# Attention scores of a prompt as fp32r products over 128 rows, with the high and low parts of queries and keys stacked in the halves of the array, in one layer of a hybrid decoder

## The chip, the cores and the metric

The kernel runs on one core of a Trainium2 chip. The metric is the time of one execution on the device in microseconds (us). Five engines appear in the profile: TensorE (PE, with its weight loads as PEld), VectorE (DVE), ScalarE (ACT), GpSimd (POOL) and SyncE (SP). SP and POOL also issue most of the DMA transfers. L135 in a row of the profile is line 135 of the kernel.

## The reference

One inference step of one trunk layer, all in float32: 512 prompt tokens and 8 x 8 sample tokens of width 1024, so 576 columns in all. Cut to what matters:

```python
h = _rmsnorm(x, norm1_g) * (1.0 + sc1) + sh1           # sc, sh, g: silu(c) @ w_ada + b_ada
proj = h @ w_in                                        # B, C, x, q, k, v, two gates
u = c_gate * xa
uc, new_conv = _causal_conv(u, conv_buf, conv_w)
ya = (b_gate * uc) @ w_conv_out
o, k_state, v_state = attend(q, k, v, attn_sinks)      # window 128, 4 key heads x 4 query heads of 64
yb = o @ w_attn_out
mixed = sigmoid(ga) * ya + sigmoid(gb) * yb
x = x + g1 * (mixed @ w_mix_out)
h2 = _rmsnorm(x, norm2_g) * (1.0 + sc2) + sh2
a, val = split(h2 @ w_up); ac, new_ffn = _causal_conv(a, ffn_buf, ffn_conv_w)
x = x + g2 * ((gelu(ac) * val) @ w_down)               # y = final norm of x

# inside attend, prompt, for each block of 128 queries against its own and the previous block of keys:
s = einsum('...qhgd,...khd->...hgqk', q, k) * HEAD_DIM ** -0.5
s = s - slopes * dist                                  # masked outside the window
m = max(max(s), sink); p = exp(s - m); p = p / (sum(p) + exp(sink - m))
o = einsum('...hgqk,...khd->...qhgd', p, v)
```

The change concerns the first line of attend for the prompt: sums over 64 channels of a head.

## The kernel before

The kernel is one Tile program. A scheduler places the instructions of each engine with a timing model of its own, except those of engines that are pinned to the order in which they are written: PE is pinned from ahead of the attention to the end, ACT and DVE from the fifteenth job (`N_ATT`) on. Helpers record most instructions in one place, so most rows have line 135.

**Large products.** A float32 product is made of three fp32r products: each operand is split into a high part (ACT copies to fp32r, `whi`, `hh`) and a low part (DVE subtracts, `wlo`, `hl`), and high·high, high·low and low·high are added in PSUM. After the first normalisation, the keys and the first query tile (`kT`; the first query tile bears that name too), and the value projection `V`, the rest of the input projection and all later products form a list of jobs. A job has seven parts of 12 products of 128x288, accumulated in the PSUM banks `bx`, `bz` and `by`, in the order bx, bz, by, bx, by, bz, by. Three of the early jobs (1, 4 and 7) give the remaining query tiles. The weights come from DRAM in `raw` tiles (a ring of four, loaded by SP). For the second block of a job the low part is made without DVE: ACT copies the high part negated, and a DMA on POOL's queue adds `raw` to it (`wlo<-raw`). Most other tiles, `kT`, queries, scores, `pt`, and the modulation weights `ada`, live in one pool of 54 buffers; a tile takes the place that came free, and its writer waits for the readers of the tile before it.

**Attention runs as filler.** `attention` is a generator that `beside_conv` advances between the pieces of the jobs' products (`tick`, .28 of a step at each). It goes through 16 units (key head `hd`, block `i`). A unit has two pairs of query heads (x = 0, 1); a tile of queries and a tile of keys hold two heads each, in rows 0 to 63 and 64 to 127 (e = 0, 1). `prompt_scores` writes the scores, adds the distance term (DVE) and ends with the softmax (DVE and ACT). Two units later `prompt_turn` transposes the probabilities (`pt`), and with every second unit `prompt_values` multiplies the `pt` of two units with `V` (L1191). Behind the values stand products for the second half of the modulations: `Modulations.sums` takes four `ada` tiles at a time (`side_by_side`, L1290, `rows<-ada,cT`). A head's units do not begin before `ready`, that is `Q_TICKS` pieces after its queries are there.

In the program's names a product is written out<-moving,stationary. The scores before:

```python
for x in range(2):
    for e in range(2):
        matmul(
            S[e][:, x * 256 : x * 256 + w], QS[2 * hd + x][HALF[e], i * P : i * P + P],
            keys(hd, e)[:, k0 : k0 + w], start=True, stop=True,
        )
```

These are four plain float32 products with 64 rows, w = 256 keys wide (128 for the first block of a head). Keys must be in the same half as the queries, so `kX` holds the two key tiles with their halves swapped, by four DMAs on POOL's queue (L941). On that queue lie, ahead of the attention, also the stores of the last keys and values (L919 to L930), the sinks (`snk`, L969) and the loads of the filters and the final gain (`par`, L999).

Of the kernel before, what the change touches and what calls it, by code (L numbers as in the profile page):

```python
# [10 lines left out]
F32 = mybir.dt.float32  # L11
F32R = mybir.dt.float32r
AF = mybir.ActivationFunctionType
ALU = mybir.AluOpType
AX = mybir.AxisListType

P = 128
D = 1024
NK = D // P
SEQ = 512  # L20
# [10 lines left out]
MOD_AHEAD = 7  # L31
MOD_TICKS = 6
N_ATT = 14
Q_TICKS = 8
OPS_AT = 1, 2, 3, 4
CACHE_AT = 17
EPS = 1e-6
# [38 lines left out]
def step_kernel(ctx: ExitStack, tc: tile.TileContext, ins: dict, outs: list):  # L76
    nc = tc.nc
# [35 lines left out]
    def slot(s, dt=F32, shape=None):  # L113
        return ap_.tile(shape or [P, NT], dt, tag="a", name=nm(s))
# [7 lines left out]
    def aux():  # L122
        return pa.tile([P, 512], F32, tag="aux", name=nm("aux"))
# [18 lines left out]
    matmul, transpose = pe.matmul, pe.transpose  # L142
# [6 lines left out]
    def pv(t):  # L149
        return t[:, 0:512]  # L150
# [10 lines left out]
    def split(hi, lo, src):  # L161

        act.activation(hi, src, AF.Copy)
        dve.tensor_tensor(out=lo, in0=src, in1=hi.bitcast(F32), op=ALU.subtract)
# [47 lines left out]
    ticks = [0]  # L212
# [347 lines left out]
    par = cp.tile([88, P], F32, tag="par", name="par")  # L560
# [302 lines left out]
    kT = []  # L863
    for j in (2, 0, 1):
        t = slot("kT")
# [21 lines left out]
    for raw in raws:  # L887
        hi = wp.tile([P, 4, 256], F32R, tag="whi", name=nm("whi"), bufs=S_BUFS)
        lo = wp.tile([P, 4, 256], F32R, tag="wlo", name=nm("wlo"), bufs=S_BUFS)
# [31 lines left out]
    for i in (3, 4):  # L921
# [3 lines left out]
        t = slot("kout", shape=[P, 256])  # L925
# [9 lines left out]
    qS = slot("qS", shape=[P, 2, 2, 4, 2, 2, 8])  # L935
    qX = slot("qX", shape=[P, 2, 2, 4, 2, 8])

    KX = [slot("kX", shape=[P, 512]) for _ in range(2)]
    for x, t in zip(KX, kT):
        for par in range(2):  # L940
            nc.gpsimd.dma_start(x[HALF[1 - par]], pv(t)[HALF[par]])  # L941

    def keys(hd, par):

        return (kT if par == hd % 2 else KX)[hd // 2][HALF[par]]

    def queries(t, q):

        hd, g2 = t // 2, t % 2
        for par in range(2):  # L950
            mine = HALF[par]
            dst = qS[:, hd // 2, :, :, par, g2, :] if par == hd % 2 else qX[:, hd // 2, :, :, g2, :]
            nc.vector.tensor_copy(
                out=dst[mine], in_=sv(q)[mine].rearrange("p (q b t) -> p q b t", q=2, b=4)
            )
        QS[t] = q
        ready[hd] = ticks[0] + Q_TICKS
        if g2 == 1:
            par = 1 - hd % 2
            for q in range(2):  # L960
                nc.gpsimd.dma_start(
                    qS[HALF[1 - par], hd // 2, q, :, par, :, :].rearrange("p b g t -> p b (g t)"),
                    qX[HALF[par], hd // 2, q].rearrange("p b g t -> p b (g t)"),
                )
# [3 lines left out]
    tc.keep_in_program_order(  # L968
        nc.gpsimd.dma_start(snk, ins["attn_sinks"][0, :].partition_broadcast(P))  # L969
    )  # L970
    queries(0, q0)
    w_q1 = weights(kpm(w_in, Q0 + P), NK)
    nd = V[2][:, 1, :]
# [172 lines left out]
    def prompt_scores(hd, i):  # L1146
        w = 256 if i else P
        k0 = (i - 1) * P if i else 0
        ss = [slot("s", shape=[P, 2, 256]) for _ in range(2)]
        S = [aux() for _ in range(2)]  # L1150
        for x in range(2):
            for e in range(2):
                matmul(
                    S[e][:, x * 256 : x * 256 + w], QS[2 * hd + x][HALF[e], i * P : i * P + P],
                    keys(hd, e)[:, k0 : k0 + w], start=True, stop=True,
                )
        for x in range(2):
            for e in range(2):
                nc.vector.scalar_tensor_tensor(
                    out=ss[x][:, e, :w], in0=nd[:, 256 - w : 256],  # L1160
                    scalar=2.0 ** (-8.0 * (4 * hd + 2 * x + e + 1) / 16),
                    in1=S[e][:, x * 256 : x * 256 + w], op0=ALU.mult, op1=ALU.add,
                )
        softmax(ss, 4, snk[:, 4 * hd : 4 * hd + 4], nsnk[:, 4 * hd : 4 * hd + 4], w)
        return ss
# [40 lines left out]
    def attention(sums):  # L1206
        units = [(hd, i) for hd in range(4) for i in range(4)]
        s, pts = {}, {}
        for n in range(len(units) + 3):
            if n == CACHE_AT:  # L1210
                cache_load(0)
            if n < len(units):
                hd, i = units[n]
                while 2 * hd + 1 not in QS or ticks[0] < ready[hd]:
                    yield False
                s[n] = prompt_scores(hd, i)
            if n >= 4 and n % 2 == 0:
                prompt_values([(*units[u], pts.pop(u)) for u in (n - 4, n - 3)])
                sums()
            yield False  # L1220
            if 2 <= n <= len(units) + 1:
                pts[n - 2] = prompt_turn(units[n - 2][1], s.pop(n - 2))
            yield False
        filler[1] = .45
        before = None
        for n in range(3):
            s, more = [], []
            if n < 2:
                yield from decode_scores(n, s, more)
            if before is not None:  # L1230
                yield from before
            before = decode_values(n, s, more)
# [1090 lines left out]
```

## Time and profile before

| what | value |
|---|---|
| median of three runs | 966.89 us (966.0 to 967.5) |
| profiled execution | 964.89 us, of which the span is 963.1 us |
| PE busy | 943.6 us (98% of the span), 7346 instructions |
| DVE, ACT, POOL busy | 723.9, 571.9 and 141.1 us |
| units of scores | between 75 and 330 us of the span, beside the jobs |

The page names for each engine its busy time, its share of the span and its number of instructions, then the span in 40 slices, the DMA queues, the chain of waits that ended last, the costliest groups of instructions and the DMA issues. A float32 product appears as two records, an fp32r product as one. The ends of products on PE are modelled, so the starts of successive products say more than the durations. All numbers of a trace come from the one profiled execution; the runs' times are taken apart from it.

### The profile page before, as it was taken

Reading aid. Unit: us, or ns where it says so; the run is one execution under the profiler, and the core shown is the slowest. Engines: PE = TensorE matmul, PEld = TensorE weight load, DVE = VectorE, ACT = ScalarE, POOL = GpSimd, SP = SyncE. Lnnn points to the kernel's source line nnn. Section 1 sums busy time; section 2 is a strip of 40 time slices with the busy share of each in tenths; the row PEclk is TensorE's granted clock in tenths of the full one; section 3 lists DMA queues with packets and bytes.
Section 4 is the critical chain, followed back from the end, with each engine's and each line's share of the span. In section 5 each row is a group of like instructions: output and inputs, shape, how many; then the busy total and the mean of one; then the engine's idle time right before and its main releaser. Section 6 shows DMA issues by size and latency. Waiting matters only on the chain.

```text
span 963.1 us, 18913 instructions
## 1 busy us (share of the span) xinstructions
PE 943.6 (98%) x7346; PEld 900.1 (93%) x7346; DVE 723.9 (75%) x1368; ACT 571.9 (59%) x1088; POOL 141.1 (15%) x320
## 2 busy tenths in 40 slices
PE   6999999999999999999999999999999999999997
PEld 5799889798889998999999999999999999999997
DVE  5687977787767558776778688995559998868864
ACT  5366686666556655686555567563226565546664
POOL 2131112021111212212001131100000000001110
PEclk9999999999999999999999999999999999999999
DMA  9987577755675888999466732332333333328542
GB/s 276 329 266 191 150 217 201 240 134 156 189 216 121 191 216 232 240 247 254 155 197 159 175 96 67 88 109 68 108 90 88 88 89 100 93 69 178 135 95 99
DMA packets 194635, 154.32 MB, mean 160 GB/s; under 512 B 7896, under 2 KB 178716, under 8 KB 194258
## 3 DMA queue, kind: packets, MB, share of 16 engines
q1 hardware_dynamic: 181890, 113.81, 39.9%
q0 software_dynamic: 11360, 36.94, 17.7%
q10 hardware_dynamic: 1296, 2.36, 0.7%
q8 instruction: 57, 0.93, 0.4%
q14 instruction: 32, 0.26, 0.1%
HBM read 115.98 MB, written 14.17 MB: 135 GB/s over the span
## 4 chain that ended last, share of the span: by engine, by line
PE 93%; DMA 3%; ACT 2%; DVE 1%; SPq 1%; issue 1%; ACTq 0%; DVEq 0%
PE mm L135 34%; PE aux L135 25%; PE by L135 13%; PE bx L135 9%; PE bz L135 8%; PE rows L1290 2%; PE aux L1191 1%; DMA ad<-in_w_ada 1%; SPq L552 1%; DMA wlo<-raw 1%; DMA x<-in_x_prompt 0%; ACT whi L135 0%; ACT wlo L135 0%; ACT s L1030 0%; DVE g L135 0%
## 5 line engine op out<-in xcount | busy, mean ns | idle before, releaser
L135 ACT ACTIVATE whi<-raw 128x1024 fp32r<-128x1024 f32 (+3 forms) x192 | 194.7, 1023 | 113.9 <-PE bz L135 36.9
L135 DVE TENSOR_TENSOR wlo<-raw,whi 128x1024 fp32r<-128x1024 f32 (+3 forms) x153 | 180.6, 1185 | 30.6 <-ACT whi L135 28.6
L135 DVE TENSOR_TENSOR raw<-raw 128x512 f32<-128x512 f32 x100 | 70.1, 701 | 2.5
L135 PE MATMUL aux<-2h,whi 128*128 128x288 f32 (+2 forms) x232 | 68.6, 296 | 0.0
L135 PE MATMUL aux<-2h,wlo 128*128 128x288 f32 (+2 forms) x232 | 68.5, 295 | 0.0
L135 PE MATMUL aux<-2l,whi 128*128 128x288 f32 (+2 forms) x232 | 68.4, 295 | 0.0
L135 POOL DMA_DIRECT2D wlo<-raw x39 | 34.4, 882 | 184.8 <-ACT p L135 59.7
L135 PE MATMUL bx<-hh,whi 128*128 128x288 f32 x184 | 55.8, 303 | 0.0
L135 PE MATMUL bx<-hl,whi 128*128 128x288 f32 x184 | 54.4, 296 | 0.0
L135 PE MATMUL bx<-hh,wlo 128*128 128x288 f32 x184 | 54.3, 295 | 0.0
L135 PE MATMUL mm<-fh,whi 128*128 128x256 f32 x224 | 47.8, 295 | 0.0
L135 PE MATMUL mm<-fh,wlo 128*128 128x256 f32 x224 | 47.7, 294 | 0.0
L135 PE MATMUL mm<-fl,whi 128*128 128x256 f32 x224 | 47.1, 292 | 0.0
L135 PEld LDWEIGHTS aux<-2h,whi 128*128 128x128 f32 x232 | 43.6, 188 | 0.0
L135 PEld LDWEIGHTS aux<-2l,whi 128*128 128x128 f32 x232 | 43.6, 188 | 0.0
L135 PEld LDWEIGHTS aux<-2h,wlo 128*128 128x128 f32 x232 | 43.5, 188 | 0.0
L135 DVE SCALAR_TENSOR_TENSOR y<-pad,par2T,y 128x592 f32<-128x592 f32 x44 | 36.6, 833 | 9.0 <-ACT y L135 8.2
L135 ACT ACTIVATE wlo<-whi 128x1024 fp32r<-128x1024 f32 (+1 forms) x39 | 40.0, 1025 | 0.8
L135 PE MATMUL by<-t,whi 128*128 128x288 f32 x184 | 39.0, 303 | 0.9 <-ACT by L135 0.9
L135 DVE SCALAR_TENSOR_TENSOR x<-mm,modT,x 128x512 f32<-128x512 f32 (+2 forms) x26 | 17.2, 663 | 28.8 <-PE mm L135 28.8
L135 PE MATMUL bz<-t,whi 128*128 128x288 f32 x184 | 38.6, 300 | 0.0
L135 PEld LDWEIGHTS mm<-fh,whi 128*128 128x128 f32 x224 | 37.2, 188 | 0.2 <-ACT nh L135 0.2
(430 smaller groups left out, 3265.5 us busy)
## 6 DMA issues: line engine op xcount, KB each, us to landing
raw<-in_w_in SPq DMA_DIRECT2D x52, 512.0 KB, 5.0
raw<-in_w_up SPq DMA_DIRECT2D x44, 512.0 KB, 3.9
wlo<-raw POOLq DMA_DIRECT2D x33, 512.0 KB, 4.7
ada<-in_w_ada SPq DMA_DIRECT2D x64, 256.0 KB, 5.2
ad<-in_w_ada SPq DMA_DIRECT2D x32, 256.0 KB, 6.4
raw<-in_w_down SPq DMA_DIRECT2D x16, 512.0 KB, 4.0
sg_dram<-sg POOLq DMA_DIRECT2D x16, 288.0 KB, 5.6
gt<-sg_dram SPq DMA_DIRECT2D x16, 288.0 KB, 5.0
```

The lines of the kernel that those rows point to most:

```text
L135: done = getattr(self.engine, name)(*args, **kwargs)
L552: return tc.keep_in_program_order(nc.sync.dma_start(dst, src))
L1191: done = nc.tensor.matmul(O[HALF[par], c], vt(i - nkt + 1 + kt)[:, hd * 64 : hd * 64 + 64], pts[kt][:, par * 256 : par * 256 + 256], start ...
L1290: done = nc.tensor.matmul(ps[32 * j : 32 * j + 32, :], cT[:, k, :], cols[j][:, k % 2, :], start=(k == 1), stop=(k == NK - 2),)
```

## The change

The scores become fp32r products over all 128 rows. The keys of a head are split into a high and a low part, and each part is written to both halves of a tile (`key_parts`: for two heads six DMAs on POOL's queue in place of two, and the `kX` tiles go). The queries are split too, and high and low are stacked: `qh` holds the high part of the even head above its low part, `qo` that of the odd head (three DMAs for each tile of queries). A product of a stacked query tile with the high keys then gives (high + low)·high, one with the low keys (high + low)·low, and both are added in PSUM. A unit has eight such products in place of four plain ones, its scores stand in one PSUM tile for each x, and the parts of the second pair of key heads are made after the sixth unit. `Q_TICKS` goes from 8 to 10.

```diff
--- before.py
+++ after.py
@@ -31,7 +31,7 @@
 MOD_AHEAD = 7
 MOD_TICKS = 6
 N_ATT = 14
-Q_TICKS = 8
+Q_TICKS = 10
 OPS_AT = 1, 2, 3, 4
 CACHE_AT = 17
 EPS = 1e-6
@@ -935,25 +935,36 @@
     qS = slot("qS", shape=[P, 2, 2, 4, 2, 2, 8])
     qX = slot("qX", shape=[P, 2, 2, 4, 2, 8])
 
-    KX = [slot("kX", shape=[P, 512]) for _ in range(2)]
-    for x, t in zip(KX, kT):
-        for par in range(2):
-            nc.gpsimd.dma_start(x[HALF[1 - par]], pv(t)[HALF[par]])
-
-    def keys(hd, par):
-
-        return (kT if par == hd % 2 else KX)[hd // 2][HALF[par]]
+    KS = {}
+
+    def key_parts(j):
+
+        parts = [slot("k", F32R, [P, SEQ]) for _ in range(4)]
+        split(parts[0], parts[1], pv(kT[j]))
+        for x in range(2):
+            src, dst = (t.bitcast(F32) for t in (parts[x], parts[x + 2]))
+            for half in HALF:
+                nc.gpsimd.dma_start(dst[half], src[HALF[1]])
+            nc.gpsimd.dma_start(src[HALF[1]], src[HALF[0]])
+        KS[2 * j], KS[2 * j + 1] = parts[0:2], parts[2:4]
 
     def queries(t, q):
 
         hd, g2 = t // 2, t % 2
+        hi, lo, odd = (slot(n, F32R, [P, SEQ]) for n in ("qh", "ql", "qo"))
+        nc.scalar.activation(hi, pv(q), AF.Copy)
+        nc.vector.tensor_tensor(out=lo, in0=pv(q), in1=hi.bitcast(F32), op=ALU.subtract)
         for par in range(2):
             mine = HALF[par]
             dst = qS[:, hd // 2, :, :, par, g2, :] if par == hd % 2 else qX[:, hd // 2, :, :, g2, :]
             nc.vector.tensor_copy(
                 out=dst[mine], in_=sv(q)[mine].rearrange("p (q b t) -> p q b t", q=2, b=4)
             )
-        QS[t] = q
+        h32, l32, o32 = (x.bitcast(F32) for x in (hi, lo, odd))
+        nc.gpsimd.dma_start(o32[HALF[0]], h32[HALF[1]])
+        nc.gpsimd.dma_start(h32[HALF[1]], l32[HALF[0]])
+        nc.gpsimd.dma_start(o32[HALF[1]], l32[HALF[1]])
+        QS[2 * t], QS[2 * t + 1] = hi, odd
         ready[hd] = ticks[0] + Q_TICKS
         if g2 == 1:
             par = 1 - hd % 2
@@ -968,6 +979,7 @@
     tc.keep_in_program_order(
         nc.gpsimd.dma_start(snk, ins["attn_sinks"][0, :].partition_broadcast(P))
     )
+    key_parts(0)
     queries(0, q0)
     w_q1 = weights(kpm(w_in, Q0 + P), NK)
     nd = V[2][:, 1, :]
@@ -1147,19 +1159,19 @@
         w = 256 if i else P
         k0 = (i - 1) * P if i else 0
         ss = [slot("s", shape=[P, 2, 256]) for _ in range(2)]
-        S = [aux() for _ in range(2)]
+        kh, kl = (x[:, k0 : k0 + w] for x in KS[hd])
         for x in range(2):
+            S = aux()
             for e in range(2):
-                matmul(
-                    S[e][:, x * 256 : x * 256 + w], QS[2 * hd + x][HALF[e], i * P : i * P + P],
-                    keys(hd, e)[:, k0 : k0 + w], start=True, stop=True,
-                )
-        for x in range(2):
+                q = QS[4 * hd + 2 * x + e][:, i * P : i * P + P]
+                dst = S[:, e * 256 : e * 256 + w]
+                matmul(dst, q, kh, start=True, stop=False)
+                matmul(dst, q, kl, start=False, stop=True)
             for e in range(2):
                 nc.vector.scalar_tensor_tensor(
                     out=ss[x][:, e, :w], in0=nd[:, 256 - w : 256],
                     scalar=2.0 ** (-8.0 * (4 * hd + 2 * x + e + 1) / 16),
-                    in1=S[e][:, x * 256 : x * 256 + w], op0=ALU.mult, op1=ALU.add,
+                    in1=S[:, e * 256 : e * 256 + w], op0=ALU.mult, op1=ALU.add,
                 )
         softmax(ss, 4, snk[:, 4 * hd : 4 * hd + 4], nsnk[:, 4 * hd : 4 * hd + 4], w)
         return ss
@@ -1211,9 +1223,11 @@
                 cache_load(0)
             if n < len(units):
                 hd, i = units[n]
-                while 2 * hd + 1 not in QS or ticks[0] < ready[hd]:
+                while 4 * hd + 3 not in QS or ticks[0] < ready[hd]:
                     yield False
                 s[n] = prompt_scores(hd, i)
+                if n == 5:
+                    key_parts(1)
             if n >= 4 and n % 2 == 0:
                 prompt_values([(*units[u], pts.pop(u)) for u in (n - 4, n - 3)])
                 sums()
```

The order of instructions moves as follows. On PE, a unit with 256 keys of the first head, before (`aux` is the PSUM tile, `bz` the job's own product):

```order
L135 MATMUL bz_1172<-hh_504,wlo_1120 128x288
L135 MATMUL aux_1296<-kT_663,kT_660 128x256
L135 MATMUL aux_1297<-kX_875,kT_660 128x256
L135 MATMUL aux_1296<-kT_663,q_999 128x256
L135 MATMUL aux_1297<-kX_875,q_999 128x256
L135 MATMUL bz_1172<-hh_512,whi_1119 128x288
```

and with the change, where `k_877` and `k_878` are the high and low keys of the head:

```order
L135 MATMUL by_1193<-n4h_721,wlo_1078 128x288
L135 MATMUL aux_1335<-k_877,qh_889 128x256
L135 MATMUL aux_1335<-k_878,qh_889 128x256
L135 MATMUL aux_1335<-k_877,qo_891 128x256
L135 MATMUL aux_1335<-k_878,qo_891 128x256
L135 MATMUL aux_1342<-k_877,qh_1015 128x256
L135 MATMUL aux_1342<-k_878,qh_1015 128x256
L135 MATMUL aux_1342<-k_877,qo_1017 128x256
L135 MATMUL aux_1342<-k_878,qo_1017 128x256
L135 MATMUL by_1193<-n4h_721,whi_1077 128x288
```

Four products became eight, and the unit stands 16 rows later, in the next part of the job. On POOL's queue, from the first store of values to the last of the keys, before (a DMA of `kX` moves one half of a key tile):

```order
L919 DMA out<-V_685 128x256
L941 DMA kX_875<-kT_663 64x512 x2
L941 DMA kX_876<-kT_666 64x512
L920 DMA out<-V_686 8x8x256
L941 DMA kX_876<-kT_666 64x512
L969 DMA snk<-in_attn_sinks 128x16
L999 DMA par_902<-in_ffn_conv_w 66x128
L928 DMA out<-kout_864 128x256
L999 DMA par_902<-in_final_g 8x128
L930 DMA out<-kout_870 8x8x256
```

and with the change, from the same store to the second load of `par` (`k_879` and `k_880` are the parts for the odd head):

```order
L919 DMA out<-V_685 128x256
L920 DMA out<-V_686 8x8x256
L928 DMA out<-kout_864 128x256
L930 DMA out<-kout_870 8x8x256
L980 DMA snk<-in_attn_sinks 128x16
L947 DMA k_879<-k_877 64x512 x2
L947 DMA k_880<-k_878 64x512 x2
L964 DMA qo_891<-qh_889 64x512
L966 DMA qo_891<-ql_890 64x512
L1011 DMA par_916<-in_ffn_conv_w 66x128
L1011 DMA par_916<-in_final_g 8x128
```

Both loads of `par` now stand behind all four stores, the sinks and the first six copies of keys and queries. Further on along POOL's queue, `wlo<-raw` for the job behind the second query job (`qS` are the sample tokens' queries), before:

```order
L961 DMA qS_873<-qX_874 64x4x16 x2
L135 DMA wlo_2073<-raw_1791 128x1024
L135 DMA sg_dram<-sg_2032 128x576
L135 DMA sg_dram<-sg_2033 128x576
L135 DMA wlo_2253<-raw_2030 128x1024
```

and with the change:

```order
L948 DMA k_1868<-k_1868 64x512
L964 DMA qo_2070<-qh_2068 64x512
L972 DMA qS_873<-qX_874 64x4x16 x2
L966 DMA qo_2070<-ql_2069 64x512
L965 DMA qh_2068<-ql_2069 64x512
L964 DMA qo_2080<-qh_2078 64x512
L966 DMA qo_2080<-ql_2079 64x512
L965 DMA qh_2078<-ql_2079 64x512
L135 DMA wlo_2157<-raw_1817 128x1024
```

One copy of keys and six copies of queries now stand with the sample tokens' queries ahead of the low part of that job. On SP, the issues around one load of modulation weights with the change; what is named in brackets are the queues and engines that the issue waits for:

```order
L1327 DMA ada_2475<-in_w_ada 128x2x256 [waits DMAHW5_49,PE_49]
L1327 DMA ada_2624<-in_w_ada 128x2x256 [waits DMASW4_49,DMASW3_49,DMAHW6_49,PE_49,Activation_49]
L174 DMA raw_2767<-in_w_in 128x8x128 [waits DMAHW1_49,DMASW6_49,DMAHW7_49,DVE_49,Activation_49]
```

`ada_2624` here takes the place of `pt_2525`. On PE the last reads of that place and of its neighbours, in the values of units 6 and 7:

```order
L135 MATMUL aux_2574<-k_1868,qo_2080 128x256
L1203 MATMUL aux_2599<-pt_2398,V_684 64x256 x2
L1203 MATMUL aux_2599<-pt_2405,V_685 64x256 x2
L1203 MATMUL aux_2599<-pt_2525,V_685 64x256 x2
L1203 MATMUL aux_2599<-pt_2532,V_685 64x256 x2
L135 MATMUL by_2507<-t_718,whi_2421 128x288
```

and, after the nine products of `by` that begin there and twelve of `bx`, whose last three lead this piece, the first reads of `ada_2624`:

```order
L135 MATMUL bx_2506<-hh_593,whi_2278 128x288
L135 MATMUL bx_2506<-hl_594,whi_2278 128x288
L135 MATMUL bx_2506<-hh_593,wlo_2279 128x288
L1304 MATMUL rows_3019<-ada_2624,cT 32x256
L1304 MATMUL rows_3019<-ada_2407,cT 32x256
L1304 MATMUL rows_3019<-ada_2409,cT 32x256
L1304 MATMUL rows_3019<-ada_2475,cT 32x256
```

## The prediction

> **What bounds the kernel now.** I read the page's first part, then its chain of waits, then the stretch of the span in which the prompt scores lie, then who waits for whom there.
>
> ```profile
> PE 943.6 (98%) x7346; PEld 900.1 (93%) x7346; DVE 723.9 (75%) x1368; ACT 571.9 (59%) x1088; POOL 141.1 (15%) x320
> PE 93%; DMA 3%; ACT 2%; DVE 1%; SPq 1%; issue 1%; ACTq 0%; DVEq 0%
> 75.00:330.00 255.00, 254.03 (x2063) 227.91 (x2056) 193.61 (x449) 169.88 (x409) 42.56 (x73) 1.00 0.67 184
> PE by L135 <- ACT by L135: 0.9, 1, 0.9
> PE rows L1290 <- ACT q L1544: 0.6, 1, 0.6
> ```
>
> PE carries 93% of the chain. In the stretch of the scores (third row: length, then PE, PEld, DVE, ACT and POOL busy) it is busy for 254.03 of 255.00 us at full clock, and the last two rows are the two waits that the profile finds for it around there. DVE has 61 us to spare in that stretch and ACT 85. So a microsecond taken from PE's stream is a microsecond of the span, one added is paid in full, and work on the other engines is free until PE has to wait for it. After this stretch the order is the same on all engines as before, so what is won or lost here stays.
>
> **The scores themselves.** Sixteen units, (head of keys, block): twelve against 256 keys, four against 128 (the first block of each head). The price of a wide unit now, in the timeline of PE:
>
> ```profile
> 102.07 0.29 PE L135 MATMUL bz<-t,wlo 128*128 128x288 f32 x1
> 102.30 0.48 PE L135 MATMUL aux<-kT,kT 64*128 64x256 f32 x1
> 102.30 0.48 PE L135 MATMUL aux<-kX,kT 64*128 64x256 f32 x1
> ...
> 103.36 0.53 PE L135 MATMUL bz<-t,whi 128*128 128x288 f32 x2
> ...
> 104.81 1.60 PE by L135 x12
> ```
>
> The two halves of the array start together (102.30), so the four float32 products of 64 rows go in pairs. A product of 128x288 takes 1.60 / 12 = 0.133 us in the stream (last row), so the unit takes 103.36 - 102.07 - 0.133 = 1.16 us. A narrow unit, and units with products of values (pt,V) right behind:
>
> ```profile
> 88.79 0.29 PE L135 MATMUL bz<-t,wlo 128*128 128x288 f32 x1
> 89.66 0.54 PE L135 MATMUL bz<-t,whi 128*128 128x288 f32 x2
> 117.09 0.29 PE L135 MATMUL bz<-t,wlo 128*128 128x288 f32 x1
> 117.96 1.08 PE L1191 MATMUL aux<-pt,V 128*64 128x256 f32 x8
> 181.01 0.29 PE L135 MATMUL bx<-hh,wlo 128*128 128x288 f32 x1
> 182.30 1.95 PE L1191 MATMUL aux<-pt,V 128*64 128x256 f32 x16
> 266.22 0.29 PE L135 MATMUL bz<-t,wlo 128*128 128x288 f32 x1
> 266.45 1.95 PE L1191 MATMUL aux<-pt,V 128*64 128x256 f32 x16
> ```
>
> The narrow unit takes 89.66 - 88.79 - 0.133 = 0.74 us. Products of values that stand alone begin 266.45 - 266.22 - 0.133 = 0.10 us late; behind scores this change of tile shape is paid within the scores' time. So a unit with values behind costs 182.30 - 181.01 - 0.133 - 0.10 = 1.06 us wide, and 117.96 - 117.09 - 0.133 - 0.10 = 0.64 narrow. Three wide and three narrow units are of this kind.
>
> Each new unit is eight fp32r products with a full 128x128 stationary block of queries and 256 or 128 moving columns. The wide form is in the trace (value projection, a new stationary block every time):
>
> ```profile
> 59.80 0.28 PE L135 MATMUL aux<-whi,hl 128*128 128x256 f32 x1
> 59.92 0.28 PE L135 MATMUL aux<-whi,hh 128*128 128x256 f32 x1
> 60.04 0.28 PE L135 MATMUL aux<-wlo,hh 128*128 128x256 f32 x1
> L1290 PEld LDWEIGHTS rows<-ada,cT 128*32 128x32 f32 x256 | 7.1, 109 | 6.7 <-issue 2.3 <-ACT q L1544 0.9 <-PE bz L135 0.2
> L135 PEld LDWEIGHTS aux<-whi,hl 128*128 128x128 f32 x40 | 7.5, 188 | 0.0
> 21.05 1.28 PE L135 MATMUL aux<-ident 128*128 128x128 f32 x10
> ```
>
> One starts every 0.12 us (0.118 over the row of them), so a wide unit becomes 8 x 0.118 = 0.94 us. No fp32r product with 128 columns is in the trace. From below, half the wide price, 0.06 us. From above, the plain float32 product of 128x128x128: ten records (two to a product) in 1.28 us, 0.22 us each. I take 0.11: a weight load lasts 109 ns with 32 columns and 188 with 128, so 0.82 ns a column, and 128 columns keep the load path for some 105 ns, longer than 128 moving columns can stream. A narrow unit becomes 8 x 0.11 = 0.88 us.
>
> The sum on PE: nine wide units alone, 9 x (0.94 - 1.16) = -2.0; three wide with values, 3 x (0.94 - 1.06) = -0.35; one narrow alone +0.14; three narrow with values 3 x (0.88 - 0.64) = +0.7. Together **-1.5 us**: the doubled number of products eats most of what one pass instead of two wins, because the old products ran two at a time. Bounds by the narrow price: 32 x 0.05 = 1.6 us less, or 32 x 0.11 = 3.5 us more.
>
> [...]
>
> **The copies that feed them.** Ten highs on ACT and ten lows on DVE (eight query tiles, two key tiles), all 128x512:
>
> ```profile
> L135 ACT ACTIVATE wh<-s 128x512 fp32r<-128x512 f32 x18 | 11.3, 630 | 0.0
> L135 DVE TENSOR_TENSOR wl<-s,wh 128x512 fp32r<-128x512 f32 x15 | 10.3, 687 | 8.0 <-ACT wh L135 7.9
> ```
>
> That is 6.3 us of ACT and 6.9 of DVE, against the 85 and 61 us that they have to spare: nothing on the path, unless one of them stands ahead of the negated copy that a pair product waits for, which is how the 0.9 us wait above arises; a second such wait would cost the same again. That the scores come some 24 PE rows later (Q_TICKS, and the units behind it) costs nothing either: the last modulation product is row 2640 of 6758 before and 2705 of 6823 now, with the same rows behind it.
>
> **The POOL queue.** The change issues 36 copies between halves (24 for queries, 12 for keys) in place of 4. Eight come ahead of two that PE waits for early, the loads of par (filters and final gain), which PE transposes at 75.31:
>
> ```profile
> 67.53 0.66 POOL L920 DMA_DIRECT2D out<-V  x1 [0.72 <-ACT kout L926]
> 68.71 0.59 POOL L969 DMA_DIRECT2D snk<-in_attn_sinks  x1
> 70.40 0.52 POOL L999 DMA_DIRECT2D par<-in_final_g  x1
> L941 POOL DMA_DIRECT2D kX<-kT x4 | 2.1, 531 | 0.0
> DMA to landing us min/median/max: 2.4/2.4/2.4
> 75.31 0.28 PE L135 MATMUL aux<-ident,par 74*128 74x74 f32 x1
> ```
>
> The four kX copies before ran while POOL waited for V anyway; now everything but the first store stands behind that wait. From 67.53: the V store 0.66, two stores of keys 0.6 each, snk 0.59, six copies at 0.53 (3.2), the first par 0.58: the second par is issued at about 73.8 and lands 2.4 us later, at 76.2. PE is there at 75.31: it waits **0.9 us** (none if two of these copies go out faster, 1.5 if the landing counts from the end of the issue). Behind PE's transpose nothing is late next, since the first scores come a job later.
>
> **A load that comes too late.** More tiles live in the pool of 54 buffers, so loads take over places that were freed later. The load ada_2624 (modulation weights) has the place of pt_2525, which the values of units 6 and 7 read as their third product. After it PE has one more product pair (four of the 16 records of 1.95 us, 0.45) and 21 products of 0.133 us (2.8) before the modulation product that reads ada_2624 first: 3.2 us. The load takes longer; the first row is over all 64 of these loads, the second over six at 176 to 200 us:
>
> ```profile
> DMA to landing us min/median/max: 2.8/5.2/7.8
> ada<-in_w_ada SPq DMA_DIRECT2D x6, 256.0 KB, 5.1
> ```
>
> PE is pinned to its order, so it waits 5.1 - 3.2 = **1.9 us** (0 with the shortest landing, 4.6 with the longest), and every later product with it. Counted the same way, the tightest such place before had 7.4 us, and PE did not wait there; now the next after this one have 6.0 and 6.8, which 5.2 still fits.
>
> **Sum.** -1.5 + 0.9 + 1.9 = +1.3 us. The profiled execution took 964.89 us (span 963.1), so it would take 966.2; the median of the three runs, 966.89, lies 2.0 above it, and I carry the difference over: **968.2 us**.
>
> **Rivals.** 0.2% is 1.9 us, about what a measurement of this kernel can tell from no change; below 965.0 is faster, above 968.8 slower.
> (1) Weight loads of 128 columns hide, the narrow product costs 0.06 us, and the ada load lands in its shortest time. For it: in all the wide rows the load costs nothing. Against it: the load's 0.82 ns a column. Then -3.1 + 0.9 = -2.2, 964.7 us, and 963.8 if the par load is in time too. [...]
> (2) No such waits, the narrow product at 0.11: -1.5, 965.4 us, no change. For it: in 255 us the trace before has only two waits of PE.
> (3) Slower: below 256 columns fp32r is charged like plain float32, 0.22 us. For it: no product of the kernel with fp32r has fewer than 256 columns, so no row contradicts it; against it: nothing but the load's figure. +3.5: 971.7 us. It decides from 0.15 us a product on.
> (4) Slower: the moved lows (the subtraction by DMA that makes the low parts of every job's second weight block) come late. In the three jobs that follow a query job the order now has them behind the new copies, some 3.6, 4.2 and 4.5 us of products ahead of their first reader on PE, where before no place had less than 7.
>
> ```profile
> wlo<-raw POOLq DMA_DIRECT2D x33, 512.0 KB, 4.7
> ```
>
> With 0.9 us to issue and 4.7 to land that would be 2.0, 1.4 and 1.1 us of waiting, +4.5: 972.7 us. Against it: the two highs on ACT that they wait for can run some 2 us before the place where they stand, as the profile before shows ACT idle between jobs. It decides if POOL is still waiting for a copy's landing when ACT is done.
>
> **How the numbers follow.** The forecast 0.50 (its own range 966.2 to 970.2; some 0.28 of it within 0.2%, 0.22 above), (1) 0.18 (0.16 of it faster), (2) 0.10, (3) 0.12, (4) 0.10. So faster 0.16, same 0.40, slower 0.44. The range of 964.5 to 972.5 leaves out the lower half of (1) and the upper halves of (3) and (4).
>
> **What would show it.** Products named k,qh and k,qo starting every 0.118 us in wide units, and in narrow ones at 0.11 (0.06 is rival 1, 0.22 rival 3). A wait of PE for the par load near 75 us, and one at the modulation products after the third value group of the third head, for an ada load. Waits of PE at the second part (bz) of a job, for wlo, would be rival 4. I am wrong in kind if PE's waits between 75 and 330 us stay under 1 us while the time rises, or if the units are gone from 1.16 to well under 0.9 us.

## The result and the profile after

The change is slower: 983.04 us in the median of four runs (981.83 to 984.0), beside 966.52 us (966.0 to 967.5) before, a ratio of 1.0169 with a 95% interval of 1.0151 to 1.0187. The forecast was 968.2 us with a range of 964.5 to 972.5, so it was wrong by 14.8 us. Nearly all of the loss lies in the stretch of the scores: the first product behind the attention (bx<-xh) starts at 433.4 us, before at 413.5. The profiled execution of the change took 984.0 us (span 982.2), 19.1 us of span more than the one before.

The first part of the page, the first row of the chain of waits, and the stretch of the scores (start and end, length, then PE, PEld, DVE, ACT and POOL busy, granted clock, share of the DMA engines, GB/s), all of the change:

```profile
PE 949.8 (97%) x7346; PEld 910.9 (93%) x7346; DVE 730.0 (74%) x1378; ACT 577.8 (59%) x1098; POOL 158.2 (16%) x352
PE 77%; DMA 12%; ACT 4%; issue 4%; DVE 3%; SPq 0%; POOL 0%; ACTq 0%; POOLq 0%
75.00:330.00 255.00, 239.43 (x1885) 220.03 (x1886) 190.15 (x443) 162.69 (x392) 56.06 (x96) 0.97 0.72 188
```

PE carried 93% of the chain before and carries 77% now; DMA went from 3% to 12%. In the stretch of the scores PE, busy for 254 of 255 us before, now stands idle for 15.6 us, and its mean clock is 0.97. The waits of PE from 60 to 345 us (in all, how many, the longest):

```profile
PE rows L1304 <- DMA ada<-in_w_ada: 9.9, 4, 4.1
PE by L135 <- ACT bz L135: 2.5, 2, 1.3
PE rows L1304 <- ACT q L1558: 1.4, 1, 1.4
PE by L135 <- ACT by L135: 1.3, 2, 0.8
PE aux L135 <- DMA par<-in_final_g: 1.1, 1, 1.1
PE by L135 <- DVE sg L135: 0.5, 1, 0.5
```

Together 16.7 us where there were 1.5. After the large ones the products run at half speed for a while. Windows of the change behind the waits that end at 161.37 and 236.63 us:

```profile
161.00:166.00 5.00, 4.63 (x28) 3.35 (x29) 3.17 (x8) 1.00 (x2) 1.56 (x3) 0.50 0.53 115
236.00:241.00 5.00, 4.37 (x28) 3.09 (x28) 0.00 (x0) 0.53 (x1) 0.00 (x0) 0.50 0.68 208
```

A product of 128x288 starts every 0.24 us there, where it otherwise starts every 0.133, so nearly half of 4.63 and of 4.37 us is lost. The half clock goes on beyond these windows, to 166.8 and 241.9 us: some 2.4 us lost each time, and some 1.4 us in the same way behind the wait for par near 78 us. So the account of the 19.1 us is, as an estimate from these rows: waits +15.2, half clock about +6.2, the scores themselves -1.4 (next), 20.0 in all. That is 0.9 us more than measured, and the ends of products are modelled.

The scores cost what was forecast. A narrow and a wide unit in the change's timeline of PE:

```profile
96.86 0.30 PE L135 MATMUL bx<-hh,wlo 128*128 128x288 f32 x1
97.00 0.34 PE L135 MATMUL aux<-k,qh 128*128 128x128 f32 x2
...
97.84 0.35 PE L135 MATMUL bx<-hh,whi 128*128 128x288 f32 x1
...
102.56 0.30 PE L135 MATMUL by<-n4h,wlo 128*128 128x288 f32 x1
102.69 0.40 PE L135 MATMUL aux<-k,qh 128*128 128x256 f32 x2
...
103.65 0.30 PE L135 MATMUL by<-n4h,whi 128*128 128x288 f32 x1
```

103.65 - 102.56 - 0.133 = 0.96 us for the wide one (forecast 0.94, before 1.16) and 97.84 - 96.86 - 0.133 = 0.85 us for the narrow one (forecast 0.88, before 0.74). With these prices the prediction's sum on PE gives -1.4 us.

How a load comes to be late is seen in the change's chain of waits from 135 to 162 us (start, length, what):

```profile
135.72 7.57 DMA sg_dram<-sg
...
143.31 0.59 ACT pt L1190
143.90 1.97 ACT s L1042 x8
...
145.97 0.95 ACT whi L135
...
147.73 0.30 ACT bz L135
...
148.07 1.87 PE by L135 x12
...
150.88 10.44 DMA ada<-in_w_ada
...
161.37 1.93 PE rows L1304 x16
```

A tile of probabilities (pt) gets its place only when the store of sg has left it, 7.6 us after its issue. On ACT the softmax (s, 143.90), the split weights (whi, 145.97) and a copy that PE waits for (bz, 147.73) come one after the other behind it, all late. Soon after, a modulation load is issued at 150.88, and PE needs it at 157.7. By this chain it lands 10.4 us after its issue, where these loads took 5.2 us in the median and at most 7.8 before; with 5.2 it would have come in time. From 150 to 155 us the DMA engines have a busy share of 1.07, in the kernel before 0.33. So this wait has two causes, a late place and a slow transfer; what slows the transfer is not shown. The longest wait, which ends at 236.63, has another history:

```profile
231.21 0.99 ACT s L1042 x5
...
232.36 4.22 DMA ada<-in_w_ada
```

Here the transfer takes 4.2 us, but the load goes out only when the softmax on ACT is done with a place, and PE stands from 232.5 us on. What SP does around the first of these waits, in its timeline of the change, then its own waits from 60 to 345 us in the change, and in the kernel before:

```profile
140.68 5.88 SPq L1327 DMA_DIRECT2D ada<-in_w_ada  x1
146.75 3.96 SPq L174 DMA_DIRECT2D raw<-in_w_in  x2
150.88 9.74 SPq L1327 DMA_DIRECT2D ada<-in_w_ada  x4
```

```profile
SPq L174 <- DMA wlo<-raw: 99.2, 14, 13.7
SPq L1327 <- PE aux L1203: 17.9, 4, 6.4
SPq L1327 <- PE aux L135: 17.6, 7, 6.7
```

```profile
SPq L174 <- DMA wlo<-raw: 165.8, 17, 13.4
SPq L1313 <- PE aux L1191: 4.7, 1, 4.7
```

Before, SP mostly waited for the ring of raw (165.8 us), and yet PE waited only 1.5 us in all, never for ada. Now modulation loads wait on SP for a place whose last reader on PE is not done (17.9 and 17.6 us), and what is queued behind them goes out late: the raw loads at 146.75 us stand behind a modulation load whose row on SP lasts 5.88 us, further modulation loads behind those.

### The profile page after: what moved, and what is told of

Read it like the earlier page. It is cut to its first block, busy times and chain, and to the rows that moved or that the text cites. A ratio compares the mean times of both kernels' runs of the same rounds, so it can differ in the third digit from the quotient of the medians.

```text
span 982.2 us, 19013 instructions
## 1 busy us (share of the span) xinstructions
PE 949.8 (97%) x7346; PEld 910.9 (93%) x7346; DVE 730.0 (74%) x1378; ACT 577.8 (59%) x1098; POOL 158.2 (16%) x352
## 4 chain that ended last, share of the span: by engine, by line
PE 77%; DMA 12%; ACT 4%; issue 4%; DVE 3%; SPq 0%; POOL 0%; ACTq 0%; POOLq 0%
PE mm L135 29%; PE aux L135 23%; PE by L135 11%; PE bx L135 6%; PE bz L135 6%; DMA ada<-in_w_ada 4%; DMA ad<-in_w_ada 2%; DMA sg_dram<-sg 2%; DMA wlo<-raw 2%; PE rows L1304 1%; ACT s L1042 1%; PE aux L1203 1%; ACT whi L135 1%; DMA raw<-in_w_in 1%; DMA raw<-in_w_down 1%
```

## The experiments

Two theories at first. PLACES: the new tiles (four for two key heads, two for each query tile) leave too few of the 54 places. QUEUE: the 32 additional copies on POOL's queue and their traffic are what makes loads and stores late. Later a third, ORDER: the scheduler puts raw and modulation loads into another order on SP's queue, and that order is slow. The ratios are to runs of the kernel before on the same chip (965.4 to 967.2 us in the median). Differences between an experiment and the change are of runs on different occasions, so differences of up to 2 us there mean little.

### Fewer places, and more copies, in the kernel before

```diff
-A_BUFS = 54
+A_BUFS = 50
```

> The kernel before with 50 places in the large pool instead of 54, nothing else. Theory PLACES (what costs the time is that the new tiles leave fewer free places, so modulation loads are issued late, SP's queue stands behind them and PE waits for the loads): 8 to 16 us slower than before (975 to 983), with PE waits on the modulation loads (rows <- DMA ada) of 5 us or more. Theory QUEUE (what costs the time is the 32 additional copies on POOL's queue and their traffic, which delay the stores of sg and the moved lows): no copies are added here, so 966 to 968 and no wait on ada above 1 us.

974.0 us, ratio 1.0078 (1.0049 to 1.0107). Slower by 7.8 us, but with one wait of 3.8 us for ACT and none for ada; what the rest went to is not shown. So places cost time, by another way than expected.

```diff
...
+        for n in range(3):
+            nc.gpsimd.dma_start(spare[12 + 3 * t + n], pv(q)[HALF[n % 2]])
         QS[t] = q
...
```

> The kernel before with 32 additional DMAs of 64x512 on POOL's queue, at the places where the change has its own (2 and 6 beside the keys, 3 after each query tile), from the keys and queries to a scratch tensor in DRAM, so that no place of the pool is taken. Theory QUEUE: 8 to 16 us slower than before, with waits of PE for wlo or for ada in the stretch of the scores. Theory PLACES: within 2 us of before (965 to 969), and PE waits under 2 us in that stretch.

964.6 us, ratio 0.9982 (0.9966 to 0.9998), PE's waits in the stretch 1.5 us in all. QUEUE falls as the cause by itself: the same number of copies in the same places of the program, to DRAM instead of to tiles, costs nothing. Whether the copies slow a load that is already late, as the one at 150 us above, is not shown.

### Single parts of the change undone

```diff
-Q_TICKS = 10
+Q_TICKS = 8
```

> The change with Q_TICKS at 8 as before. Theories PLACES and QUEUE: little moves, 979 to 985, since the number of tiles and copies stays; if the later start of a head's units (their queries hold places longer) is what matters, 4 us or more faster than the change (979 or less).

983.1 us, ratio 1.0173. The later start of the units does not explain the loss. The single waits are not the same, though: PE has one wait on ada of 5.2 us here, in place of four of 9.9 in all.

```diff
-                if n == 5:
+                if n == 7:
                     key_parts(1)
...
-        if n == 5:
+        if n == 7:
             mark = cp.tile([P, 1], F32, tag="mark", name="mark")
             x1_after = pool.tensor_copy(out=mark, in_=t[:, 0:1])
...
-        if n == 5:
+        if n == 7:
             stF = state_in(st_ffn, "stF", NF)
```

> The change with the parts of the second pair of key heads made after the eighth unit instead of the sixth, so that four tiles live two units shorter, beside the parts of the first pair. Theory PLACES: 4 to 10 us faster than the change (973 to 979), the waits on ada near 161 and 189 us shorter. Theory QUEUE: the same copies two units later, 981 to 985.

995.4 us, ratio 1.030. The run does more than its expectation says: far behind the attention, in the loop that mixes the two branches, the edit also moves two steps from the sixth to the eighth round, a mark that lets the load of x go and the state of the second convolution. Up to the first product behind the attention the later keys gained nothing (it starts at 435.8 us, in the change at 433.4), against what PLACES expected: the wait near 161 us was gone, but those near 188 and 239 us stayed (4.3 and 4.5 us). The rest is a wait of 8.1 us for wlo that ends at 550 us, and the chain puts it down to the load of x, which now goes out late on POOL's queue, ahead of that wlo:

```profile
536.62 0.55 DMA x<-xT_dram
...
537.70 12.72 DMA wlo<-raw
```

So 995.4 us is no measure of the later keys.

```diff
-S_BUFS = 5
+S_BUFS = 4
-A_BUFS = 54
+A_BUFS = 57     (second run only)
```

> The change with rings of four split weights instead of five (S_BUFS), 54 places in the large pool. It is the base for the next run, which has three more places. A shorter ring can only make the split weights later: 983 to 990.

> The change with rings of four split weights and, in the memory that this frees, 57 places in the large pool. SP's loads stand in nearly the same order as in the run before. Theory PLACES (the loads are late because they wait for a place): 5 us or more faster than that run, and the waits on ada shorter by as much. Theory ORDER (the loads are late because SP's queue has them behind loads of raw, which wait for the landing of wlo): within 3 us of that run, the waits on ada the same.

1098.6 and 1089.6 us. Three more places were worth 9 us, but with a ring of four split weights PE waits for wlo in the stretch of the scores (12.6 and 13.8 us) and for copies on ACT all through the later stages, up to 3.9 us a time. The waits on ada up to 400 us were 4.6 us in the first and 5.1 in the second. This pair tells nothing on how the loads come late.

```diff
-MOD_AHEAD = 7
+MOD_AHEAD = 8
```

> The change with up to eight modulation loads ahead instead of seven (MOD_AHEAD), so that the fourth load of a group no longer waits for the group before it, at the price of one more place. Theory ORDER: the loads stand earlier on SP's queue, waits on ada under 3 us, 5 us or more faster than the change (978 or less). Theory PLACES: no gain, 981 to 987, since one more tile wants a place.

985.9 us, waits on ada still 10.7 us. One load more ahead does not help while it needs a place.

```diff
+    par2 = cp.tile([74, P], F32, tag="par2", name="par2")
+    for dst, src in (...):
+        ... nc.gpsimd.dma_start(dst, src)
     key_parts(0)
     queries(0, q0)
```

> The change with the two loads of par issued ahead of the copies of keys and queries on POOL's queue. If the wait for par and the half clock behind it are what the early stage costs: the 1.1 us wait near 78 us goes, PE's clock stays at 1.00 there, and 2.5 to 3.5 us are won against the change (979.5 to 980.5). If the half clock has another cause, only the wait goes: 981.5 to 982.

983.2 us, no gain. The early wait and its half clock did go; the same window of the change, then of this kernel:

```profile
78.00:81.00 3.00, 2.72 (x12) 2.75 (x13) 2.99 (x5) 1.62 (x2) 3.00 (x6) 0.51 0.92 252
```

```profile
78.00:81.00 3.00, 3.00 (x31) 2.26 (x31) 3.00 (x5) 2.68 (x6) 3.00 (x6) 1.00 0.99 256
```

At the first by of the job PE is 3.8 us ahead of the change (79.85 against 83.69 us, 0.6 of it from ahead of this stage). Twelve microseconds later that is gone, in this kernel's timeline and in the window behind it:

```profile
91.75 0.40 PE L135 MATMUL bz<-t,wlo 128*128 128x288 f32 x1 [1.76 <-DMA wlo<-raw]
```

```profile
92.00:95.00 3.00, 3.00 (x15) 3.00 (x15) 0.00 (x0) 0.78 (x2) 0.07 (x1) 0.53 1.13 330
```

The moved low that PE waits for is issued at 83.5 us in both kernels. In the change PE comes to it late and needs no wait; here it comes on time, waits 1.8 us and pays the half clock again. At 95.8 us it is 0.4 us ahead of the change, and the longest wait on ada ends at 236.54 us, in the change at 236.63. What PE won at one transfer it spent at the next.

### The dose, half of the change, and two other forms of the scores

```diff
-A_BUFS = 54
+A_BUFS = 53
```

> The change with 53 places in the large pool instead of 54. Theory PLACES: one place fewer where the change already waits for places costs 3 to 10 us (986 to 993). If it is the order of the loads or the copies and not the places: within 3 us of the change (980 to 986).

988.5 us, ratio 1.0219 (1.0184 to 1.0253), some 5 us slower than the change, as PLACES expected. But the loads on SP stand in a slightly other order than in the change, and the two intervals touch; e18 below keeps the order.

In the next run the new branch is used for key heads 0 and 1 only (in `queries` for the first four tiles), and the other heads keep the old one:

```diff
+        if hd < 2:
             kh, kl = (x[:, k0 : k0 + w] for x in KS[hd])
...
+        else:
+            S = [aux() for _ in range(2)]
...
-                if n == 5:
-                    key_parts(1)
```

> The change for key heads 0 and 1 alone; heads 2 and 3 keep the plain float32 products of 64 rows with one swapped key tile, so that four key parts and one tile per later query tile are not made. Theory PLACES: the waits on ada from 150 us on fall to 2 us or less in all, 966 to 972 (the early loss of some 4 us stays). If any half of the change brings SP's queue into the slow order: 975 or more.

985.6 us, ratio 1.0188: as slow as the whole. A wait of 5.2 us on ada stands at 236.8 us, where this kernel holds no more tiles than the kernel before. Its load is issued at 231.98 us, right behind a load of raw on SP (231.67). PLACES alone does not explain that.

```diff
+            for n, (a, b) in enumerate(((0, 0), (1, 0), (0, 1))):
+                for e in range(2):
+                    matmul(S[e][...], QS[2 * hd + x][a][HALF[e], ...], KS[...][b][HALF[e], ...],
+                           start=n == 0, stop=n == 2)
```

> Scores from the same number of parts as in the change (four key tiles for two heads, two tiles for a query tile), but as three fp32r products of 64 rows (high.high, low.high, high.low), the halves side by side: no copies of queries, 8 copies of keys, Q_TICKS 8, second keys after the eighth unit. If fp32r products of 64 rows run in pairs like the plain ones, a wide unit takes 6 x 0.118 = 0.71 us and PE saves some 5 us against before. Theory PLACES: the time does not follow PE, 972 to 985, with waits on ada. Without PLACES: 960 to 966.

981.3 us, but with waits on ada of only 0.7 us, though it holds as many tiles as the change. The first product behind the attention starts at 420.2 us, 6.7 later than in the kernel before and 13.2 earlier than in the change; its longest wait up to there is for ACT near 82 us (3.0). The rest came behind the stretch, in waits of 2.4 and 7.1 us, and the second is that of e4: this edit moves the same two steps of the mixing loop. So of its loss some 7 us belong to the scores. Its loads stand on SP nearly in the order of the kernel before. That brought up ORDER. Its unit, in the timeline of PE:

```profile
101.43 0.29 PE L135 MATMUL bz<-hh,wlo 128*128 128x288 f32 x1
101.65 0.39 PE L135 MATMUL aux<-k,qh 64*128 64x256 f32 x2
101.87 0.29 PE L135 MATMUL aux<-k,ql 64*128 64x256 f32 x2
101.99 0.41 PE L135 MATMUL aux<-k,qh 64*128 64x256 f32 x4
...
102.56 0.40 PE L135 MATMUL bz<-hh,whi 128*128 128x288 f32 x1
```

102.56 - 101.43 - 0.133 = 1.00 us for twelve fp32r products of 64 rows. From the second pair on a pair starts every 0.12 us (101.87, 101.99, where the row holds two pairs), so they do run in pairs, at the price of one product of 128 rows (0.118 us before), and six pairs take some 0.7 us. The other 0.3 us go at the two ends of the unit, where the rows go from `128*128` to `64*128` and back: 0.22 us from the last bz to the first pair, 0.22 to the second pair, and 0.21 from the last pair to the next bz. The plain unit has some 0.3 us over too: its four pairs start 0.21 us apart, and it takes 1.16 us. The expectation left these 0.3 us out.

The next kernel makes the parts for each unit, in two tiles that live for that unit:

```diff
...
+        k, q = (slot(n, F32R, [P, 2, 256]) for n in ("kp", "qp"))
+        for e in range(2):
+            src = keys(hd, e)[:, k0 : k0 + w]
+            nc.scalar.activation(k[HALF[e], 0, :w], src, AF.Copy)
+            nc.vector.tensor_tensor(out=k[HALF[e], 1, :w], in0=src, in1=..., op=ALU.subtract)
...
```

> The kernel before (keys and swapped keys, one tile per query tile) with Q_TICKS 7 and high and low parts made for each unit just ahead of it, in two tiles that live for a unit only; products as in the run before (three of 64 rows, side by side). ACT and DVE get four small operations each per unit (some 20 us each in all, beside PE). Theory PLACES: hardly any place is taken, so the waits stay as before and PE's gain of some 5 us is seen: 960 to 964. If the halves do not run side by side, a wide unit takes 12 x 0.118 = 1.42 us: 969 to 972. If the small operations come late, PE waits ahead of the scores.

975.0 us, ratio 1.0076 (1.0050 to 1.0102): 8 us better than the change, but slower than before, with one wait on ada of 3.7 us.

### The order of loads by itself

The next kernels keep raw, modulation and cache loads on SP in a given order, by edges that fix only the order of issue (`in_line` around the three kinds of loads). In the kernel before, a typical stretch of that order is raw raw ada ada raw ada ada raw ada raw raw ada ada; in the change it is raw raw ada raw raw ada ada ada ada raw raw ada raw.

```diff
+    LOADS = "RRRRRaaaaRRRaaaRRRRRaaaRRaaRaaRaRRaaRaaRaaRaaRRRaaRaRaaaRaaRaaaRcccc..."
...
-        nc.sync.dma_start(raw, src)
+        in_line("R", nc.sync.dma_start(raw, src))
...
```

> The change, with raw, modulation and cache loads kept on SP's queue in exactly the order that they have in the kernel before (edges of order only, no waits). Theory ORDER (a modulation load stands behind raw loads whose ring waits for the landing of wlo): the waits on ada from 120 us on fall under 2 us in all, 966 to 972. Theory PLACES (the tiles take the places, whatever the order): the waits stay, 978 or more, or move to waits for raw's products.

974.9 us, ratio 1.0099 (1.0072 to 1.0125), 8 us faster than the change. The waits of PE in the stretch that are left, first rows:

```profile
PE by L135 <- ACT by L135: 3.3, 3, 2.0
PE by L135 <- ACT bz L135: 1.8, 2, 1.2
PE rows L1332 <- DMA ada<-in_w_ada: 1.7, 1, 1.7
```

On ada 1.7 instead of 9.9 us, and 11.9 us in all instead of 16.7. Of these, 4.4 us lie ahead of 84 us: for ACT's q (1.4), for par (1.0) and for by (2.0); the kernel before has 0.6 there. Its runs lie between 972.6 and 978.4; in the profiled one, near the lower end, the clock was 1.00 from 75 to 330 us.

The same edit to the kernel before, with the order of the change:

```diff
+    LOADS = "RRRRRaaaaRRaaaRRRRRRaaaRRaRRaaaaRRaRaaRaaRaaRaRRRaRaaaaaaRaRaaaRcccc..."
...
```

> The kernel before, with the order of loads on SP's queue that the change has, from the first modulation load to the last cache load of the scores' stage. Nothing else. Theory ORDER: slower than before by 6 to 16 us (973 to 983) with waits on ada. Theory PLACES: within 2 us of before.

978.5 us, ratio 1.0124 (1.0104 to 1.0144): 11.8 us lost with no new product, tile or copy. Its chain of waits shows how:

```profile
217.74 5.95 DMA wlo<-raw
...
223.82 0.37 SPq L202
...
224.28 4.49 DMA ada<-in_w_ada
...
228.81 1.94 PE rows L1318 x16
```

SP holds a raw load (L202) until the moved low of an older raw tile has landed, at 223.69 us; the modulation load stands behind it and goes out at 224.28. PE waits 3.7 us for it. Its other waits in the stretch are mostly for the copy bz on ACT, 4.0 us in three times.

The edits of e13 and e8 together:

> As the run e13, and the loads of par ahead of the copies of keys and queries. Theory ORDER: the early loss of some 4 us (par, and the half clock behind it) goes too and is not given back at a later wait: 3 to 5 us faster than e13, 962 to 968. Theory PLACES: no faster than e13, as in e8.

976.2 us, ratio 1.0103: no better than e13. Waits of 2.6 us for sg near 88 us and 2.8 on ada at 187 us took the place of the one for par.

The edits of e12 and e13 together:

> As e12 (parts made for each unit, products of 64 rows side by side at 1.00 us a wide and 0.90 a narrow unit), with the loads on SP's queue in the order of the kernel before. Theory ORDER: the 3.7 us wait on ada and its half clock go, 4 to 7 us faster than e12: 967 to 971. Theory PLACES: as e12, 973 to 977.

970.5 us, ratio 1.0042 (1.0027 to 1.0056), 4.5 us faster than e12. The clock is 1.00 from 60 to 345 us, and no wait on ada is left. What is left from 100 to 340 us is small waits, 5.1 us in all, the largest part for the copy bz on ACT (2.1 in three times) and for x on DVE (1.5 in two).

The split operations on ACT and DVE are not free after all. No version was found that beats the kernel before.

### Places by themselves, at the same order

The kernel before, with its own order kept:

```diff
-A_BUFS = 54
+A_BUFS = 50
```

> The kernel before with 50 places and its own order of loads on SP's queue kept (e1 had 50 places and a slightly other order, +7.8 us). If places cost by themselves: 970 or more, with a wait near 148 us as in e1. If they cost only by the order that they bring about: within 2 us of before.

974.5 us, ratio 1.0088 (1.0073 to 1.0103). With the order of loads kept, four places fewer still cost 9 us. (e1, without the edges of order, lost 7.8, so the edges themselves cost little.) Its chain of waits:

```profile
133.78 6.81 DMA sg_dram<-sg
...
144.25 2.07 ACT s L1058 x8
...
147.14 1.04 ACT whi L135
148.18 0.30 ACT bz L135
...
148.53 1.57 PE by L135 x5
```

It is the chain that the change shows at 135 us: a tile of the attention waits for the place of an sg whose store is under way; softmax, weights and the copy bz follow late on ACT; PE waits 3.9 us.

The kernel of e13:

```diff
-A_BUFS = 54
+A_BUFS = 53
```

> As e13 (the change with the old order of loads, 974.9) with 53 places. If places cost by themselves: 3 us or more slower than e13 (978 or more). If only by the order: within 3 us of e13 (972 to 978).

984.7 us, ratio 1.0202 (1.0178 to 1.0227), 9.8 us slower than e13 by one place. Places cost by themselves (e17, e18), and so does the order (e14). The two do not simply add up: with 53 places the old order gives 1.0202 and the change's own 1.0219 (e9), no difference beyond the intervals, so the 8 us of e13 hold for 54 places.

## Why the prediction was wrong

**What bounds the kernel.** It was right that PE bounded the kernel before, and wrong that this would hold after: DMA goes from 3% to 12% of the chain, and in e8 the 3.2 us that PE won early were lost 12 us later at a wait for a transfer.

**The scores.** The term of -1.5 us stands, at -1.4: 0.96 and 0.85 us a unit, against 0.94 and 0.88. Rivals (1) and (3) fall with the narrow price of about 0.85 / 8 = 0.106 us. The forecast had 0.11 us there, the rivals 0.06 and 0.22.

**The POOL queue.** The wait for par was 1.1 us against 0.9, in part by luck: the second par was issued at 74.64 us (forecast 73.8) and landed at about 78.2 (forecast 76.2), and PE came at 77.2 instead of 75.3, so both sides were some 2 us late. That copies cost nothing otherwise fits e2. Rival (4) did not come in the change, where PE has no wait for wlo in the stretch; it was close, as e8 shows with 1.8 us.

**A load that comes too late.** Here the prediction failed. The mechanism was right, more tiles in the pool make modulation loads late, but the place and the size were not: the load at ada_2624 had no wait, and four others had 9.9 us in all instead of 1.9 (the products that read ada_2624 first start at 202.71 us, right behind those before them). I priced each load by itself, from the release of its own place to its first reader, and took the next tightest places (6.0 and 6.8 us) as safe. The runs showed two things in the place of that: a load can be held up by what stands ahead of it on SP's queue (e14, where the modulation load went out at 224.28 us behind a raw load held to 223.82; 11.8 us by the order alone), and a place can be held by a store, which then delays the softmax, the weights and the copy bz behind it on ACT (e17, a store of 6.81 us; 9 us by places alone). Undoing the order gives back 8 of the change's 16.5 us (e13). The other 8 are not taken apart in full: one place less costs e13 9.8 us more (e18), which points to the places, and 3.8 us of e13's waits are the early work below.

**The half clock.** Missing from the sum altogether: some 6.2 us, an estimate. The rows 161 to 166 and 236 to 241 us show it at 0.50, behind waits of 3.7 and 4.1 us, and the row 78 to 81 at 0.51, behind waits of 1.4 and 1.1 us (for ACT's q and for par).

**The copies that feed the scores.** "Nothing on the path" was too simple. The waits on ACT's q and by near 75 to 84 us, when the splits of keys and first queries are made beside the first jobs, are part of the change's loss. From the last transposes of keys (68.0 us, before 67.0) to the first by (83.69, before 78.81) the change loses 3.9 us; the prediction had 0.9 there. With par ahead of the copies (e8) the same piece loses only 0.7 us, so most of it hangs on the wait for par and the half clock behind it. Later, e16 shows small waits on ACT and DVE adding up where the places and the order are as before; how much that is by itself in the change stays open.

**Rival (2)**, no waits at all, was the opposite of what came. No rival held a time above 972.7.

## What to carry to other kernels

In a kernel whose buffers are full, a new tile is not free because its engine has time: count what waits for the places (one place less cost 9.8 us in e18), and follow each queue in its order, since a load that is held can put off those behind it. After an edit compare the order of the loads first; an order that changed by itself can cost more than the edit brings (11.8 us in e14, against 1.4 won by the scores). And a wait of PE is to be priced with the half clock that may stand behind it, in the change 1.4, 2.4 and 2.4 us more at three places, by the estimate above.

## What the runs showed of the hardware that was not expected

- Pairs of fp32r products of 64 rows and 256 columns in the two halves start every 0.12 us in e11, as products of 128 rows do (0.118). A unit of six pairs still takes 1.00 us, some 0.3 us more than its pairs, at its two ends, where the shape of the tile changes; the plain unit has about as much over (1.16 us). Side by side therefore wins 0.16 us a unit; the stacked unit has no change of shape and takes 0.96 us.
- An fp32r product of 128 rows with 128 columns costs about 0.106 us in the change's narrow unit (0.85 us for eight), hardly less than the 0.118 with 256 columns.
- From 75 to 345 us the granted clock of the change is 0.50 in three stretches, 78.0 to 81.5, 160.0 to 166.8 and 235.1 to 241.9 us, and 1.00 between them; in the kernel before it is 1.00 all the way. Not all idle time of PE was followed by half clock. The first row below, right ahead of 160.0 us, has 2.25 us of idle time. The second has 1.65 us, in waits of 1.1 us for ada and 0.5 for sg, and the clock stays at 1.00 behind it:

```profile
156.56:159.97 3.41, 1.16 (x9) 0.93 (x8) 2.82 (x10) 2.35 (x10) 2.10 (x4) 1.00 1.15 229
187.29:190.70 3.41, 1.76 (x22) 0.87 (x20) 1.02 (x3) 1.06 (x1) 0.58 (x1) 1.00 0.94 291
```

In e13 a wait of 2.0 us for by is not followed by it either (1.00 from 75 to 330 us), while in the change waits of 1.4 and 1.1 us shortly after one another are. What sets these cases apart is not shown.
